# Gate and up projections by Strassen's seven products, and the out projection over two token tiles at a time

## The chip, the cores and the metric

The kernel runs on one core of one Trainium2 chip. The metric is the time of one execution on the device, in microseconds (us). The engines are TensorE (PE, with PEld for its weight loads), VectorE (DVE), ScalarE (ACT), GpSimd (POOL) and SyncE (SP), whose queue issues all DMA transfers here.

## The reference

One decoder layer for 512 tokens of width 1024, all in float32: attention and a gated recurrence are merged, then a feed-forward block. The change lies in the last three lines:

```python
merged = merge_g[:, :, 0] * (attn @ w_o_attn) + merge_g[:, :, 1] * (lru @ w_o_lru)
x = x + merged @ w_out
h2 = _rmsnorm(x, norm2_g)
return x + (jax.nn.silu(h2 @ w_gate) * (h2 @ w_up)) @ w_down
```

`w_out` is 1024 x 1024, `w_gate` and `w_up` are 1024 x 2816, `w_down` is 2816 x 1024.

## The kernel before

A float32 product is made of three matmuls of a narrower type. Each operand is split into a high part, which is the operand rounded by an ACT cast, and a low part, which is a subtraction of operand and high part; `mm3` (L193) issues high x high, high x low, low x high into one PSUM bank.

Weights come as packed chunks of 128 x 1024 (512 KB) in the order of `weight_chunks` (L65). `W.load` (L138) issues their DMA on SP into a `raw` buffer, `W.cut` (L170, L148) makes `whi` on ACT (L164) and `wlo` on DVE (L167), and `W.get` (L174) hands one over and keeps later chunks cut and loaded ahead. Everything stands in program order on each engine; nothing reorders it at run time.

The tail has three stages. The **out projection** (L1161 to L1172) keeps eight banks, four token tiles of 128 times two halves of 512 columns, and runs over the eight chunks of `w_out`; the last three chunks go token tile by token tile, so that `norm2_sums` (L1128: x added, squares on ACT, gain on POOL), `norm2_scale` (L1140) and `norm2_t` (L1147: transposes and split into `h2q`) of one tile lie beside matmuls of the next. The **gate and up projections** (L1183 to L1210) run over 22 row tiles of 128 features; each has one chunk of `w_gate` and one of `w_up`, and each chunk is multiplied with all 512 tokens in 8 x 3 matmuls of 512 columns (`mm_cm`, L283; the first three chunks take the tokens in halves of 256). Silu on ACT, the product on DVE (L1205) and a split (L1209) make the operands of the **down projection** (L1212 to L1232). Its 22 pairs stay in SBUF, as does the sum x2.

In this stage DVE and ACT make the parts two chunks ahead of PE, and POOL has nothing to do.

Of the kernel before, what the change touches and what calls it, by code (L numbers as in the profile page):

```python
# [64 lines left out]
def weight_chunks():  # L65
# [19 lines left out]
    L += [cols("w_out", ((0, D),), k, 1) for k in range(KT)]  # L85
# [14 lines left out]
def hybrid_block_kernel(ctx: ExitStack, tc: tile.TileContext, x: bass.AP, wpk: bass.AP,  # L100
# [997 lines left out]
    def late_pool(**kw):  # L1098
        p_, es = open_pool(**kw)
        ctx.enter_context(es)  # L1100
        return p_

    stage3 = late_pool(name="stage3", bufs=3, side="right")
    x2p = late_pool(name="x2p", bufs=1)
    h2p = late_pool(name="h2p", bufs=1)
    gp = late_pool(name="gp", bufs=28)
    fp = late_pool(name="fp", bufs=2, side="right")
    ps = late_pool(name="ps_ffn", bufs=8, space=PSUM)
    PS.clear()
    PS.update(b=8)  # L1110
    W.stage((stage2, stage3, stage3, stage2, stage3), (stage2, stage3), (dve,))
    x2 = x2p.tile([P, NT, D], F32, name="x2")
    for t in range(NT):
        nc.sync.dma_start(x2[:, t, :], x[t * P:(t + 1) * P, :])

    def wkey(name, h, c):
        return cols(name, ((512 * h, 512 * h + 512),), 2 * c, 2)

    h2q = [[h2p.tile([P, 4, T], F32R, name=f"h2{m}{b}") for m in "hl"] for b in range(2)]
    h2T = [[m[:, k % 4, :] for m in h2q[k // 4]] for k in range(KT)]  # L1120
    xn2, sums = {}, {}
# [24 lines left out]

    def norm2_t(t):  # L1147
        for b in range(2):
            pt = bank("b")
            for kk in range(4):  # L1150
                pe.transpose(pt[:, kk * P:(kk + 1) * P], xn2[t][b][:, kk * P:(kk + 1) * P], ident)
            split(*[m[:, :, t * P:(t + 1) * P] for m in h2q[b]], pt.rearrange("p (k n) -> p k n", n=P))

    acc = [[bank("b") for _ in range(2)] for _ in range(NT)]
# [28 lines left out]
    gT = []  # L1183
    units = [(n, i) for i in range(FT) for n in ("w_gate", "w_up")]
    early = 3
    w, acc = [], []
    for n, i in units[:early]:
        w.append(W.get(cm(n, P * i), KT, ahead=0))
        acc.append(bank("b"))
        mm_cm(acc[-1], w[-1], h2T, lo_half, between=(lambda: norm2_t(len(w))) if len(w) > 1 else None)  # L1190
    gate_acc = None
    for n, (name, i) in enumerate(units):
        if n < early:
            a = acc[n]
            mm_cm(a, w[n], h2T, hi_half)
            W.cut(W.used)
        else:
            a = bank("b")
            mm_cm(a, W.get(cm(name, P * i), KT, ahead=2), h2T)
        if name == "w_gate":  # L1200
            gate_acc = a
            continue
        sg = fp.tile([P, T], F32, tag="sg", name="sg")
        act.activation(sg, gate_acc, AF.Silu)
        dve.tensor_tensor(out=sg, in0=sg, in1=a, op=OP.mult)  # L1205
# [89 lines left out]
```

## Time and profile before

| | |
|---|---|
| runs of the kernel | 1012.01, 1012.25, 1012.58 us; median 1012.25 |
| the profiled execution | 1012.1 us, its span 1010.0 us |
| PE busy in the span | 981.0 us (97%) |
| DVE, ACT, POOL busy | 570.5 us (56%), 458.6 us (45%), 223.1 us (22%) |
| mean granted TensorE clock | 0.998 of full speed |
| DMA | 100.65 MB, mean 100 GB/s |

The span runs from the first to the last instruction of one profiled execution; the 2.1 us around it belong to the execution's time. Busy times are shares of that span, averaged over stages that differ: what a change in one stage is worth must be read there. A matmul's duration in the rows includes the time in which it overlaps the next one, so the pace of matmuls is read from their starts.

### The profile page before, as it was taken

What the parts mean: (1) busy time and instruction counts of PE and PEld (TensorE: products, weight loads), DVE (VectorE), ACT (ScalarE), POOL (GpSimd) and SP (SyncE); (2) the same over time, 40 slices, a digit from 0 to 9 for tenths busy, and PEclk for the clock granted to TensorE, in tenths of its full rate; (3) what the DMA queues carried; (4) which work ended last, traced back from release to release, by engine and by line L of the source; (5) the groups of instructions that cost most, each with busy time, mean ns of one, the idle gap of its engine ahead of it and who ended that gap; (6) DMA issues with size and microseconds to landing.
All of it is one profiled execution on the core that took longest, in us unless ns stands there. A gap on an engine that the chain in (4) does not pass through costs nothing.

```text
span 1010.0 us, 13183 instructions
## 1 busy us (share of the span) xinstructions
PE 981.0 (97%) x4915; PEld 817.0 (81%) x4915; DVE 570.5 (56%) x1053; ACT 458.6 (45%) x867; POOL 223.1 (22%) x271
## 2 busy tenths in 40 slices
PE   6999997799999999999999999999999999999998
PEld 5878876588898888778888888988888888888887
DVE  5777679746766787887875544623322332231311
ACT  6544565336545777776773334523222322231210
POOL 1031148713201555645542002200000000000000
PEclk9999999999999999999999999999999999999999
DMA  5322324642213111322113464132332233232401
GB/s 190 105 84 83 123 84 138 196 148 92 90 56 116 63 53 43 105 84 64 33 63 99 151 254 132 45 122 84 88 119 86 83 92 117 84 125 63 167 21 42
DMA packets 32175, 100.65 MB, mean 100 GB/s; under 512 B 3696, under 2 KB 4080, under 8 KB 32112
## 3 DMA queue, kind: packets, MB, share of 16 engines
q1 hardware_dynamic: 32112, 99.82, 30.7%
q8 instruction: 38, 0.62, 0.2%
q14 instruction: 25, 0.20, 0.1%
HBM read 91.42 MB, written 8.39 MB: 99 GB/s over the span
## 4 chain that ended last, share of the span: by engine, by line
PE 86%; DVE 7%; ACT 3%; issue 2%; DMA 2%; POOL 0%; ACTq 0%; DVEq 0%
PE ps_b L197 14%; PE ps_b L198 14%; PE ps_b L196 14%; PE ps_dense L1006 9%; PE ps_dense L198 5%; PE ps_dense L197 5%; PE ps_dense L196 5%; PE ps_t L880 3%; PE ps_s L197 2%; PE ps_s L196 2%; PE ps_s L198 2%; DVE wlo L167 2%; PE ps_s L849 2%; PE ps_s L850 2%; PE ps_pv L908 2%
## 5 line engine op out<-in xcount | busy, mean ns | idle before, releaser
L167 DVE TENSOR_TENSOR wlo<-raw,whi 128x1024 fp32r<-128x1024 f32 (+2 forms) x199 | 193.6, 989 | 114.0 <-ACT whi L164 113.6
L164 ACT CAST whi<-raw 128x1024 fp32r<-128x1024 f32 (+2 forms) x207 | 166.0, 819 | 136.8 <-PE ps_b L198 69.1
L196 PE MATMUL ps_b<-h2h,whi 128*128 128x512 f32 (+1 forms) x376 | 143.4, 381 | 0.0
L198 PE MATMUL ps_b<-h2h,wlo 128*128 128x512 f32 (+1 forms) x376 | 143.2, 381 | 0.0
L197 PE MATMUL ps_b<-h2l,whi 128*128 128x512 f32 (+1 forms) x376 | 143.2, 381 | 0.0
L198 PE MATMUL ps_dense<-hth,wlo 128*128 128x512 f32 (+1 forms) x232 | 87.9, 379 | 11.2 <-DVE wlo L167 11.2
L871 POOL TENSOR_SCALAR p<-p,st,gates 128x128 f32<-128x128 f32 (+3 forms) x128 | 80.0, 638 | 84.7 <-DVE st L867 47.2
L1205 DVE TENSOR_TENSOR sg<-sg,ps_b 128x512 f32<-128x512 f32 x22 | 15.2, 689 | 138.2 <-PE ps_b L198 138.2
L196 PE MATMUL ps_dense<-hth,whi 128*128 128x512 f32 (+1 forms) x232 | 87.4, 377 | 0.0
L197 PE MATMUL ps_dense<-htl,whi 128*128 128x512 f32 (+1 forms) x232 | 87.1, 375 | 0.0
L197 PEld LDWEIGHTS ps_b<-h2l,whi 128*128 128x128 f32 x376 | 70.7, 188 | 15.0
L196 PEld LDWEIGHTS ps_b<-h2h,whi 128*128 128x128 f32 x376 | 70.7, 188 | 14.9
L198 PEld LDWEIGHTS ps_b<-h2h,wlo 128*128 128x128 f32 x376 | 70.7, 188 | 14.8
L861 ACT ACTIVATE p<-p,st 128x128 f32<-128x128 f32 (+3 forms) x128 | 72.0, 563 | 23.0 <-DVE st L856 22.3
L197 PE MATMUL ps_b<-wlo,gh 128*128 128x512 f32 (+1 forms) x198 | 73.2, 370 | 0.0
L198 PE MATMUL ps_b<-whi,gl 128*128 128x512 f32 (+1 forms) x198 | 73.1, 369 | 0.0
L196 PE MATMUL ps_b<-whi,gh 128*128 128x512 f32 (+1 forms) x198 | 73.1, 369 | 0.0
L186 ACT CAST gh<-sg 128x512 fp32r<-128x512 f32 x22 | 13.6, 620 | 123.2 <-DVE sg L1205 123.2
L892 DVE TENSOR_TENSOR ptl<-ps_t,pth 128x512 fp32r<-128x512 f32 x80 | 55.1, 689 | 21.1 <-ACT pth L886 20.4
L856 DVE CUSTOM_DVE_ANT_0 p<-ps_s,bias 128x128 f32<-128x128 f32 (+3 forms) x128 | 61.2, 482 | 9.2 <-PE ps_s L850 6.2
L198 PEld LDWEIGHTS ps_dense<-hth,wlo 128*128 128x128 f32 x232 | 44.4, 191 | 21.7 <-DVE wlo L167 13.5
L886 ACT CAST pth<-ps_t 128x512 fp32r<-128x512 f32 x80 | 46.5, 582 | 29.7 <-PE ps_t L880 29.2
(265 smaller groups left out, 2072.8 us busy)
## 6 DMA issues: line engine op xcount, KB each, us to landing
raw<-in_wpk_dram SPq DMA_DIRECT2D x150, 512.0 KB, 3.6
mg_d<-mt SPq DMA_DIRECT2D x16, 256.0 KB, 4.3
mt<-mg_d SPq DMA_DIRECT2D x16, 256.0 KB, 3.0
xt<-in_x_dram SPq DMA_DIRECT2D x4, 512.0 KB, 5.6
lru_d<-lt SPq DMA_DIRECT2D x8, 256.0 KB, 5.6
lraw<-lru_d SPq DMA_DIRECT2D x8, 256.0 KB, 2.7
x<-in_x_dram SPq DMA_DIRECT2D x4, 512.0 KB, 6.5
out_dram<-o SPq DMA_DIRECT2D x7, 256.0 KB, 2.0
```

Of the source, the lines that this page charges most:

```text
L164: (on_hi or act.copy)(hi[:, sl], raw[:, sl])
L167: eng.tensor_tensor(out=lo[:, sl], in0=raw[:, sl], in1=f(hi[:, sl]), op=OP.subtract)
L196: pe.matmul(acc, lhsT=ah, rhs=bh, start=start, stop=False)
L197: pe.matmul(acc, lhsT=ah, rhs=bl, start=False, stop=False)
L198: pe.matmul(acc, lhsT=al, rhs=bh, start=False, stop=stop)
L856: dve.tensor_tensor_reduce(out=p, in0=accs.pop((h, br, t)), in1=bias[h][:, 384 - t * P:512], scale=-1.0, scalar=3e38, op0=OP.add, op1=OP.m ...
L861: act.activation(p, p, AF.Exp, bias=stat[h][:, 0, br, t:t + 1], scale=-1.0, accum_out=stat[h][:, 1, br, t:t + 1])
L871: pool.tensor_scalar(p, p, sm[:, t:t + 1], gates[:, t, c:c + 1], op0=OP.mult, op1=OP.mult)
L880: pe.transpose(pt[:, o_:o_ + P], probs[h, br, t][:, k * P:(k + 1) * P], ident)
L886: act.copy(ph, pts[h, gi][0])
L892: dve.tensor_tensor(out=pl, in0=pt, in1=f(ph), op=OP.subtract)
L1006: pe.matmul(acc, lhsT=a[l], rhs=b[r], start=start and i == 0, stop=stop and i == 2)
```

## The change

**Out projection.** The chunks of `w_out` are listed twice (`* 2`) and stored once. The first pass makes token tiles 0 and 1, the second 2 and 3, so a chunk is loaded and cut twice and serves 12 matmuls each time instead of 24. The norm of tiles 0 and 1 lies beside the second pass. x comes in by tile, the sum x2 is written to DRAM (`x2_d`) and read back near the end of each half of the down projection.

**Gate and up.** Two row tiles of both projections form a group `o`: four chunks, and with the contraction and the tokens halved, two-by-two blocks. A11 is row tile 0 with the first half of the contraction, A12 row tile 0 with the second, A21 and A22 the same for row tile 1; each has a gate part and an up part of 512 columns. B11 is the first half of the contraction for tokens 0 to 255, B21 the second half for them, B12 and B22 the same for tokens 256 to 511. Seven products take the place of eight. Four sums of A blocks (S1 to S4) are made per group on POOL, two additions of 512 columns each; the sums of B (T1 to T4) are made once. The products come in the order p = 1, 2, 6, 5, 7, 4, 3, with operands A11 x B11, A12 x B21, S2 x T2, S1 x T1, S3 x T3, A22 x T4, S4 x B22. `product` issues 2 x 4 x 3 matmuls of 256 columns into one bank, `prep` makes the parts of the weights three products ahead, `post` adds the banks up on DVE, and `gated` multiplies Silu's result on POOL. The third and fourth chunk hold A21 and A22, so S1 needs both.

**Down projection.** Its operands are kept whole and split into parts beside its own first half (`down_parts`).

The diff, cut to its core:

```diff
-    L += [cols("w_out", ((0, D),), k, 1) for k in range(KT)]
+    L += [cols("w_out", ((0, D),), k, 1) for k in range(KT)] * 2
...
+    W.raw_bufs = {id(stage2): 2, id(stage3): 3}
...
+    def blocks_late(t, pt):
+        t1, t2, t3, t4 = [half(f"t{i}") for i in range(4)]
+        act.copy(t1, pt[0])
+        dve.tensor_tensor(out=t3, in0=pt[1], in1=t1, op=OP.subtract)
+        pool.tensor_tensor(out=t2, in0=t3, in1=b11[t - 2], op=OP.add)
+        pool.tensor_tensor(out=t1, in0=t1, in1=b11[t - 2], op=OP.subtract)
+        pool.tensor_tensor(out=t4, in0=d0[t - 2], in1=t3, op=OP.subtract)
+        block("B22", t, pt[1])
+        block("T3", t, t3)
+        return (("T2", t2), ("T1", t1), ("T4", t4))
...
+    seq = [(o, p) for o in range(NO) for p in (1, 2, 6, 5, 7, 4, 3)]
...
+    SUMS = {"S1": ("A21", OP.add, "A22"), "S2": ("S1", OP.subtract, "A11"),
+            "S3": ("A11", OP.subtract, "A21"), "S4": ("A12", OP.subtract, "S2")}
+
+    def add_up(o, name):
+        S[o, name] = sp.tile([P, 1024], F32, tag="S", name="S")
+        a, op, b = SUMS[name]
+        for n in range(2):
+            pool.tensor_tensor(out=a_of(o, name, n), in0=a_of(o, a, n), in1=a_of(o, b, n), op=op)
+
+    def adds(s):
+        if s < len(seq):
+            o, p = seq[s]
+            for name in {6: ("S1", "S2"), 7: ("S3",)}.get(p, ()):
+                add_up(o, name)
...
+        if A_OF[p][0] == "S":
+            src = S.pop((o, A_OF[p])) if p != 6 else S[o, "S2"]
+            split(hi, lo, src)
+            if p == 5:
+                add_up(o, "S4")
+                load_upto(o, 6)
+            return
+        for n in range(2):
+            sl = slice(512 * n, 512 * n + 512)
+            split(hi[:, sl], lo[:, sl], a_of(o, A_OF[p], n))
+        if p == 4:
+            load_upto(o, 8)
+
+    def product(s):
+        o, p = seq[s]
+        banks[o, p] = b = at_bank(s % 8)
+        hi, lo = parts.pop(s)
+        bh, bl = h2[B_OF[p]]
+        for n in range(2):
+            for k in range(4):
+                sl = slice(512 * n + k * P, 512 * n + k * P + P)
+                mm3(b[:, 256 * n:256 * n + 256], (hi[:, sl], lo[:, sl]), (bh[:, k, :], bl[:, k, :]), k == 0, k == 3)
...
+    def gated(i, c):
+        sg = half("sg")
+        act.activation(sg, c[:, 0, :], AF.Silu)
+        pool.tensor_tensor(out=g_tile(i), in0=sg, in1=c[:, 1, :], op=OP.mult)
...
+        elif p == 6:
+            held[2] = half("u2")
+            add(both(held[2]), 6, 1)
+        elif p == 7:
+            held[3] = half("u3")
+            held[4] = half("u4")
+            add(both(held[3]), 7, 2)
+            add(both(held[4]), 5, 2)
+            add(corner(1, 1), 5, 3)
+        elif p == 4:
+            add(corner(1, 0), 4, 3)
+            gated(2 * o + 1, c2s.pop((o, 1)))
+        elif p == 3:
+            add(corner(0, 1), 3, 4)
+            gated(2 * o, c2s.pop((o, 0)))
...
+    for _ in range(KT):
+        k, w = w_out(2)
+        for t in (0, 1):
+            out_mm(t, k, w)
...
+    product(0)
+    post(0)
+    for n, src in late2:
+        block(n, 2, src)
+    pt = norm2_t(3)
+    product(1)
+    late3 = blocks_late(3, pt)
+    for n, src in late3:
+        block(n, 3, src)
+    AHEAD = 3
...
+    for s in range(2, len(seq)):
+        product(s)
+        adds(s + AHEAD + 1)
+        prep(s + AHEAD)
+        post(s - 1)
...
+            if h == 0:
+                for i in range(2 * c + 2, min(2 * c + 4, FT)):
+                    down_parts(i)
```

How the instructions stand now. **SP at the start of the out projection** (L1114, L1134 load x, L1126, L1128 the gain, L143, L145 chunks of weights, L1142 stores x2). Before:

```order
L143 DMA raw<-in_wpk_dram 128x1024
L1114 DMA x_6112<-in_x_dram 128x1024 x4
L1126 DMA gain_6121<-in_rows_dram 128x512
L1126 DMA gain_6122<-in_rows_dram 128x512
L143 DMA raw<-in_wpk_dram 128x1024 x64
```

and now:

```order
L1128 DMA gain_6113<-in_rows_dram 128x512
L1128 DMA gain_6114<-in_rows_dram 128x512
L1134 DMA x_6139<-in_x_dram 128x512
L1134 DMA x_6140<-in_x_dram 128x512
L1134 DMA x_6143<-in_x_dram 128x512
L1134 DMA x_6144<-in_x_dram 128x512
L145 DMA raw<-in_wpk_dram 128x1024 x10
L1142 DMA x_d<-x_6139 128x512
L1142 DMA x_d<-x_6140 128x512
L145 DMA raw<-in_wpk_dram 128x1024
```

Half of x stands ahead of the chunks instead of all of it, and stores of x2 stand between chunk loads.

**DVE on the way into the products**, from the end of token tile 2's norm to the first product that needs a sum of B (L189 is the subtract of `split`, L1184 is t3, L207 to L1154 the scaling of token tile 3):

```order
L189 TENSOR_TENSOR h2lB_6122<-ps_b,h2hB_6121 128x4x128
L189 TENSOR_TENSOR h2lT_6128<-t_6597,h2hT_6127 128x4x128
...
L1154 TENSOR_SCALAR xn_6581<-xn_6581,nsy 128x512
...
L1184 TENSOR_TENSOR t_6690<-ps_b,t_6688 128x512
L189 TENSOR_TENSOR h2lB_6122<-ps_b,h2hB_6121 128x4x128
L189 TENSOR_TENSOR h2lT_6128<-t_6690,h2hT_6127 128x4x128
L189 TENSOR_TENSOR h2lT_6126<-t_6689,h2hT_6125 128x4x128
L189 TENSOR_TENSOR h2lT_6124<-t_6688,h2hT_6123 128x4x128
L189 TENSOR_TENSOR h2lT_6130<-t_6691,h2hT_6129 128x4x128
L189 TENSOR_TENSOR wlo<-S,whi 128x1024 x3
```

Before, this stretch held four subtracts per token tile pair and no t; now the scaling of tile 3 stands behind tile 2's t (just ahead of these rows), B22 and T3, and the parts of S2, S1 and S3 behind all blocks of tile 3.

**A group of the gate and up projections.** Before, DVE had this from the second norm's last splits through the first row tile (L167 the subtract of one chunk, L1205 the gating, L187 the split of its result)

```order
L187 TENSOR_TENSOR h2l_6118<-ps_b,h2h_6117 128x4x128
L187 TENSOR_TENSOR h2l_6120<-ps_b,h2h_6119 128x4x128
L167 TENSOR_TENSOR wlo<-raw,whi 128x1024
L1205 TENSOR_TENSOR sg<-sg,ps_b 128x512
L187 TENSOR_TENSOR gl<-sg,gh 128x512
L167 TENSOR_TENSOR wlo<-raw,whi 128x1024 x2
```

that is, four rows for each row tile, and now it has for a group of two (L1292 are the additions of `post`; from S1 of one group to S2 of the next):

```order
L189 TENSOR_TENSOR wlo<-S,whi 128x1024
L1292 TENSOR_TENSOR c<-ps_b,u_6867 128x2x256
L189 TENSOR_TENSOR wlo<-S,whi 128x1024
L189 TENSOR_TENSOR wlo<-raw,whi 128x512 x2
L1292 TENSOR_TENSOR c<-ps_b,u_6978 128x2x256
L189 TENSOR_TENSOR wlo<-S,whi 128x1024
L1292 TENSOR_TENSOR u_7047<-ps_b,u_6978 128x512
L189 TENSOR_TENSOR wlo<-raw,whi 128x512 x4
L1292 TENSOR_TENSOR u_7117<-ps_b,u_7047 128x512
L1292 TENSOR_TENSOR u_7118<-ps_b,u_7047 128x512
L1292 TENSOR_TENSOR c<-ps_b,u_7117 128x2x256
L189 TENSOR_TENSOR wlo<-S,whi 128x1024
```

while POOL, which had nothing there, has ten operations (L1227 the sums, in the order S3, S4, S1 and S2 of the next group; L1282 the gating after p = 4 and after p = 3):

```order
L1282 TENSOR_TENSOR g<-sg,c 128x512
L1227 TENSOR_TENSOR S<-raw 128x512 x2
L1227 TENSOR_TENSOR S<-raw,S 128x512 x2
L1282 TENSOR_TENSOR g<-sg,c 128x512
L1227 TENSOR_TENSOR S<-raw 128x512 x2
L1227 TENSOR_TENSOR S<-S,raw 128x512 x2
```

DVE's row `wlo<-S` at the end is S2 of the next group; the addition after p = 4 stands behind it.

## Rows read from the trace of the kernel before

**Rows 1.** The page: busy time by engine (us, share, count), and the chain that ended last.

```profile
PE 981.0 (97%) x4915; PEld 817.0 (81%) x4915; DVE 570.5 (56%) x1053; ACT 458.6 (45%) x867; POOL 223.1 (22%) x271
...
PE 86%; DVE 7%; ACT 3%; issue 2%; DMA 2%; POOL 0%; ACTq 0%; DVEq 0%
```

**Rows 2.** Timeline of PE (start, us, engine, line): first and 36th matmul of 256 columns.

```profile
635.11 0.28 PE L196 MATMUL ps_b<-h2h,whi 128*128 128x256 f32 x1
...
639.25 0.28 PE L198 MATMUL ps_b<-h2h,wlo 128*128 128x256 f32 x1
```

**Rows 3.** The same: the last 15 matmuls of the gate and up projections, and the next.

```profile
880.00 0.40 PE L196 MATMUL ps_b<-h2h,whi 128*128 128x512 f32 x1
...
883.27 0.40 PE L198 MATMUL ps_b<-h2h,wlo 128*128 128x512 f32 x1
883.51 0.39 PE L196 MATMUL ps_b<-whi,gh 128*128 128x512 f32 x1
```

**Rows 4.** Groups by form, 660 to 880 us (busy us, mean ns | idle before).

```profile
L167 DVE TENSOR_TENSOR wlo<-raw,whi 128x1024 fp32r<-128x1024 f32 x40 | 47.2, 1222 | 5.3 <-ACT whi L164 5.3
L164 ACT CAST whi<-raw 128x1024 fp32r<-128x1024 f32 x40 | 39.9, 1045 | 0.0
L187 DVE TENSOR_TENSOR gl<-sg,gh 128x512 fp32r<-128x512 f32 x20 | 13.8, 692 | 13.7 <-ACT gh L186 13.7
L1205 DVE TENSOR_TENSOR sg<-sg,ps_b 128x512 f32<-128x512 f32 x20 | 13.8, 689 | 127.4 <-PE ps_b L198 127.4
L186 ACT CAST gh<-sg 128x512 fp32r<-128x512 f32 x20 | 12.4, 620 | 114.4 <-DVE sg L1205 114.4
L1204 ACT ACTIVATE sg<-ps_b 128x512 f32<-128x512 f32 x20 | 11.9, 598 | 46.9 <-PE ps_b L198 46.9
```

**Rows 5.** Timelines of POOL and DVE around 630 us.

```profile
629.79 2.54 POOL L1135 TENSOR_TENSOR xn<-x,gain 128x512 f32<-128x512 f32 x2 [1.20 <-DVE x L1132]
...
631.73 1.29 DVE L187 TENSOR_TENSOR h2l<-ps_b,h2h 128x512 fp32r<-128x512 f32 x2 [0.89 <-ACT h2h L186]
```

**Rows 6.** Timelines of POOL and DVE, 157 to 163 us, in the recurrence.

```profile
157.54 2.18 POOL L379 TENSOR_TENSOR tv<-tv,mv 128x512 f32<-128x512 f32 x1
...
158.58 2.23 DVE L167 TENSOR_TENSOR wlo<-raw,whi 128x1024 fp32r<-128x1024 f32 x1
...
160.72 2.30 DVE L167 TENSOR_TENSOR wlo<-raw,whi 128x1024 fp32r<-128x1024 f32 x1
```

**Rows 7.** PE's waits (total, times, longest), its timeline, and a window (last: clock, DMA).

```profile
PE ps_dense L198 <- DVE wlo L167: 11.2, 5, 5.1
...
160.86 0.80 PE L198 MATMUL ps_dense<-hth,wlo 128*128 128x512 f32 x1 [5.07 <-DVE wlo L167]
...
161.88 0.63 PE L197 MATMUL ps_dense<-htl,whi 128*128 128x512 f32 x1
162.30 0.63 PE L198 MATMUL ps_dense<-hth,wlo 128*128 128x512 f32 x1
...
162.00:163.00 1.00, 1.00 (x4) 0.81 (x3) 1.00 (x2) 0.00 (x0) 1.00 (x1) 0.50 0.53 49
```

**Rows 8.** DMA issues, 660 to 880 us (count, KB each, median us to landing).

```profile
raw<-in_wpk_dram SPq DMA_DIRECT2D x40, 512.0 KB, 3.9
```

**Rows 9.** Start of the out projection: timelines of PE, SP, ACT, and a window (last: GB/s).

```profile
588.57 0.40 PE L196 MATMUL ps_b<-whi,mh 128*128 128x512 f32 x1
...
591.03 0.48 SPq L143 DMA_DIRECT2D raw<-in_wpk_dram  x1
...
601.25 1.05 ACT L164 CAST whi<-raw 128x1024 fp32r<-128x1024 f32 x1 [8.52 <-DMA raw<-in_wpk_dram]
...
598.00:599.00 1.00, 1.00 (x6) 0.81 (x5) 0.00 (x0) 0.00 (x0) 0.00 (x0) 1.00 1.03 410
```

**Rows 10.** Timelines of DVE and ACT: the second norm of a token tile.

```profile
625.28 1.28 DVE L1132 TENSOR_TENSOR x<-x,ps_b 128x512 f32<-128x512 f32 x2
...
628.51 0.72 ACT L1144 ACTIVATE xn<-xn,nsy 128x512 f32<-128x512 f32 x1 [0.85 <-DVE nsy L208]
```

More of the change, by code (lines that the diff above doesn't have):

```diff
@@ L1099, in late_pool @@
         p_, es = open_pool(**kw)
[L1100 to L1121, printed above, removed]
+        return p_, es
+    stage3, _ = late_pool(name="stage3", bufs=3, side="right")
+    ctx.enter_context(_)
+    ga, _ = late_pool(name="ga", bufs=6)
@@ L1145, in norm2_scale, with block @@
         dve.tensor_scalar(xn2[t][1], xn2[t][1], y, None, op0=OP.mult)
+    NB = ("B11", "B21", "B22", "T1", "T2", "T3", "T4")
+    h2 = {n: [h2p.tile([P, 4, 2 * P], F32R, name=f"h2{m}{n}") for m in "hl"] for n in NB}
+    b11, d0 = {}, {}
+    def block(n, t, src):
+        sl = slice((t % 2) * P, (t % 2) * P + P)
+        split(*[m[:, :, sl] for m in h2[n]], src.rearrange("p (k n) -> p k n", n=P))
     def norm2_t(t):
+        pt = [at_bank(2 * t + b) for b in range(2)]
         for b in range(2):
-            pt = bank("b")
@@ L1150, in norm2_t, with blocks_early @@
             for kk in range(4):
[L1151 to L1154 removed]
+                pe.transpose(pt[b][:, kk * P:(kk + 1) * P], xn2[t][b][:, kk * P:(kk + 1) * P], ident)
+        return pt
+    def blocks_early(t, pt):
+        block("B11", t, pt[0])
+        block("B21", t, pt[1])
+        b11[t] = ga.tile([P, 512], F32, tag="g", name="b11")
+        d0[t] = ga.tile([P, 512], F32, tag="g", name="d0")
+        act.copy(b11[t], pt[0])
+        dve.tensor_tensor(out=d0[t], in0=pt[1], in1=b11[t], op=OP.subtract)
@@ L1180, in hybrid_block_kernel @@
-    norm2_scale(3)
[L1183 to L1195, printed above, removed]
-            W.cut(W.used)
[L1197 to L1205, printed above, removed]
-        pool_, tag = (gp, "g") if i < 14 else (hpool, "h")
-        hi = pool_.tile([P, T], F32R, tag=tag, name="gh")
-        lo = pool_.tile([P, T], F32R, tag=tag, name="gl")
-        split(hi, lo, sg)
-        gT.append((hi, lo))
+    for t in range(NT):
+        acc[t] = [at_bank(2 * t + h) for h in range(2)]
@@ new lines, in hybrid_block_kernel @@
+    ws = [w_out(late - 1 - i) for i in range(late)]
+    W.cut_ = W.used
+    W.load(W.used + 3)
+    prep(0)
+    prep(1)
+    for k, w in ws:
+        out_mm(2, k, w)
+    adds(2)
+    norm2_sums(2)
+    for k, w in ws:
+        out_mm(3, k, w)
+    norm2_scale(2)
+    pt = norm2_t(2)
+    norm2_sums(3)
+    late2 = blocks_late(2, pt)
+    norm2_scale(3)
+    product(0)
[5 more added lines that the diff above has]
+    late3 = blocks_late(3, pt)
```

178 lines of the change are left out of this document (143 added, 35 removed).

## The prediction

> **What bounds the kernel now.** I read the page first. TensorE is busy 97% of the span and the chain that ended last is 86% PE [rows 1]: PE sets the time, and whatever takes matmuls away pays in full as long as PE stays fed. The timeline of the gate and up projections comes next: the 512-column matmuls there start 14 steps apart from 880.00 to 883.27, 0.2336 us each, without gaps, and the stage ends at 883.51, where the down projection begins [rows 3]. Then, by form, the other engines in this stage: per weight chunk one ACT cast of 1.05 and one VectorE subtract of 1.22, and POOL has no row at all [rows 4]. So VectorE and ACT idle more than half of it, and POOL is free. The changed kernel spends that spare time.
>
> **Matmuls.** Before: 44 chunks x 8 x 3 = 1056 matmuls of 512 columns, 1056 x 0.2336 = 246.7 us. After: 11 groups x 7 products x 24 = 1848 of 256 columns. A narrow one is not quite half price: from 635.11 to 639.25 lie 35 steps of 256-column matmuls, each with weights of its own, 0.1183 us [rows 2]. 1848 x 0.1183 = 218.6 us. Saved: **28.1 us**. A product is 24 x 0.1183 = 2.84 us, a group 19.9; the same two row tiles took 22.4.
>
> **What each group now asks of the others.** DVE: four subtracts of 1024 (1.22) and six of 512 (0.69), seven additions that read a bank (0.69): 13.9 us. ACT: four casts of 1.05, six of 0.62, one copy and two Silu of 0.60: 9.7. POOL: eight additions for S1 to S4 and two gating multiplies; its nearest row, two 512-wide multiplies in 2.54, gives 1.27 each [rows 4, 5]: 12.7. DMA: four chunks as before, 2 MB in 20 us, where 410 GB/s were reached [rows 9]. By shares all fit under 19.9. Two things speak against reading it by shares.
>
> First, POOL and DVE stop each other when DVE reads two SBUF operands. From 157.5 on, POOL multiplies that alone take 1.27 take 2.2, and DVE subtracts that alone take 1.22 take 2.2 to 2.3, starting about 2.14 apart [rows 4 to 6]: they alternate, some 1.1 each. A DVE subtract that reads PSUM kept 1.29 for two beside the multiplies of 629.79 [rows 5]. So only the ten weight subtracts of a group collide, not its additions.
>
> The Trainium skill (SBUF — State Buffer, Who interferes with whom) says that two SBUF inputs on VectorE and a GpSimd read block each other for the whole instruction. The trace agrees that they alternate, but its 2.14 per pair is less than 1.22 + 1.27. At the full durations of rows 4 and 5 a group's colliding work is 12.7 + 4 x 1.22 + 6 x 0.69 = 21.7 us, more than PE's 19.9; by the row of the pair it is about 10 x 1.1 + 4 x 1.1 + 6 x 0.55 = 18.7, and no bound by itself. I take the row; the other is a rival below.
>
> Second, the sums form a ring from group to group. S4's last half frees the buffer into which the next group's third chunk is loaded; S1 needs that chunk, S2 needs S1, the subtract of S2 stands on DVE ahead of the addition after p=4 of the group under way (DVE's printed order), that addition feeds Silu and POOL's gating multiply, and behind the multiply POOL has S3 and S4. One turn without collisions: gating, S3, S4 on POOL 5 x 1.27 = 6.4; load 3.9 from issue to landing [rows 8]; S1 and S2 4 x 1.27 = 5.1; cast, subtract, addition, Silu 1.05 + 1.22 + 0.69 + 0.60 = 3.6: 19.0, just under PE's 19.9. Now the collisions. The subtract of S1 falls between gating and S3 (+1.1), that of S3 between S4's halves (+1.1); the four half subtracts for the next p=1 and p=2 become due just when S1 and S2 run (4 x 0.55 = +2.2); and DVE then reaches S2 late, with its last half and three additions still in front, less the cast that runs meanwhile (0.55 + 3 x 0.62 - 1.05 = +1.4). Off go 0.2 each for eight POOL operations whose start-up hides in the wait (-1.6). Sum 19.0 + 4.2 = **23.2 us a turn**. Bounds: 19.9 (nothing collides, PE sets it) and 24.8 (nothing hides). I take 23.2, because the row of the collision has the same two engines and operand kinds. Ten turns; the first finds S1 and S2 ready some 2 us early and the last group's own waits give about as much back, so nine count: 9 x (23.2 - 19.9) = **+30 us** (0 to 44).
>
> **Out projection and the way into the products.** Chunks now serve half as many matmuls: 2.8 us per chunk instead of 5.6, with cast and subtract of 1.05 and 1.22. That fits, except at the start. Before, the first chunk behind the x loads was issued at 591.03 and its cast began at 601.25, since x, gain and chunks were in flight at 410 GB/s [rows 9]; it was needed at 588.6 + 3 x 5.6 = 605.4. Now 1 MB of x is gone from the front (SP's printed order), so it lands 2.5 to 4 us earlier, but is needed at 597.0 and wants 1.05 + 1.22 first: **+2 us** (0 to 4).
>
> The tail of the norm was hidden under matmuls. From the first addition to the scaled row takes 625.28 to 629.23, about 4 us [rows 10]. Walked in the printed order of DVE, with every subtract at its row's price: in the second pass each early token tile's transposes wait about 1.2 us (DVE also cuts chunks there): 2.5. Token tile 2 starts its sums behind p=1's and p=2's subtracts and stalls PE some 2. Token tile 3 stands behind t, B22 and T3 of tile 2 (0.60 + 3 x 0.69) and its own scaling (1.9), and one product of 2.84 covers it: 4. Then product 3 needs T2 of tile 3 and S2's parts: copy, t, POOL's addition, seven subtracts of DVE (0.60 + 0.69 + 1.27 + 6 x 0.69 + 1.22 + collisions 1.5 = 9.4), covered by one product: 6.6. Sum **+15** (7 to 18). After such a gap the clock falls: a wait of 5.07 us for a subtract was followed by stretches at 0.50, the lower level, with matmuls at 0.43 instead of 0.23 for eight of them [rows 7]: **+1.6** (0 to 3.2).
>
> **At no cost.** The down projection's operands are now split during its first half: per chunk of 5.6 us DVE has 1.22 + 2 x 0.69, ACT 1.05 + 2 x 0.62; if its first two splits were late, up to 2 us. Spilling x2 adds 4 MB of traffic, and in SP's line stores that wait for DVE's additions with chunk loads behind them: those loads run two to four chunks ahead (5.6 us and more) and the additions take 1.3, so nothing, or up to 2. The last additions and stores are as before.
>
> **Sum** against the profiled execution, 1012.1 us (span 1010.0): 1012.1 - 28.1 + 30 + 2 + 15 + 1.6 = 1032.6, and 0.15 more for the median of 1012.25: **1033 us**, slower by 2%. A difference of 0.2%, 2 us, is about what can be told from none.
>
> **Rivals.** *The sums hide* (faster). If DVE seldom meets POOL, a group takes PE's 19.9 us and only the entry costs remain: 1012.2 - 28.1 + 2 + 13 + 1.6 = 1001. For it: the uncollided turn is under PE's time, and three products are prepared ahead. Against: rows 6, and the stretch around them, where DVE and POOL work without pause and PE waits 11.2 us for subtracts in five pieces [rows 7]. The point that decides: (28.1 - 18.6) / 9 = 1.06, so below 20.9 us a group it is faster, above slower. Chance 0.26.
>
> *The port alone sets the pace.* If colliding instructions exclude each other for their full durations and S2 is never late on DVE, a group is 21.7 us: 10 x 1.8 = 18, 1012.2 - 28.1 + 18 + 18.6 = 1021. For it: POOL's tail beside DVE is seen in one kind of pair only; against: 2.14 a pair [rows 6]. Chance 0.16. This is what the rule of the Trainium skill (SBUF — State Buffer, Who interferes with whom) would make of it.
>
> *Fewer matmuls do not follow.* The order of PE shows 168 narrow ones per group, so the work is removed; no chance is set aside.
>
> **How the numbers follow.** Forecast, group of 22 to 24.8 us, 1022 to 1048: 0.55. Port 0.16, hidden 0.26 (994 to 1009), worse than 1048 0.03. With some of the cheap end on either side of 1012: faster 0.27, same 0.04, slower 0.69. The range leaves out about 0.1 at each end: 997 to 1046; the forecast's own is 1020 to 1046.
>
> **What would show it.** Right: narrow matmuls still 0.118 apart within a product; PE waiting for DVE subtracts of S2, S1 and S3 in every group, with products of one kind 23 us apart; POOL additions of 2.2 us where a weight subtract overlaps and 1.3 elsewhere; two gaps of 4 to 7 us around the first two products, and a stretch at the lower clock. Wrong: groups 19.9 to 20.5 apart with PE over 95% busy, or subtracts and POOL additions that overlap unstretched.

## The result and the profile after

The changed kernel takes **1040.8 us** (median of four runs, 1038.96 to 1041.69) beside 1012.27 for the kernel before: ratio 1.0279, 95% interval 1.0262 to 1.0297, slower by 28.5 us. The profiled execution took 1040.92 us, its span 1038.9. The page of the changed kernel, busy time by engine and the chain that ended last:

```profile
PE 973.8 (94%) x5635; PEld 843.7 (81%) x5635; DVE 720.1 (69%) x1193; ACT 513.1 (49%) x962; POOL 408.9 (39%) x386
...
PE 60%; DVE 18%; issue 7%; POOL 6%; ACT 5%; DMA 3%; DVEq 0%; POOLq 0%; ACTq 0%
```

Beside [rows 1]: PE holds 60% of the chain instead of 86%, and DVE and POOL now hold 24%. PE's busy time hides this (981.0 before, 973.8 now): a narrow matmul counts for 0.28 us, though the next one starts 0.12 later, so a part of every gap counts as busy. Where the 28.9 us of span went is read from the starts on PE's timeline, here of the changed kernel:

```profile
588.65 0.39 PE L198 MATMUL ps_b<-whi,mh 128*128 128x512 f32 x1
...
646.43 0.56 PE L198 MATMUL ps_b<-h2hB,whi 128*128 128x256 f32 x1
...
680.10 0.28 PE L198 MATMUL ps_b<-h2hB,whi 128*128 128x256 f32 x1
...
682.98 0.28 PE L198 MATMUL ps_b<-h2hB,whi 128*128 128x256 f32 x1
...
700.26 0.28 PE L198 MATMUL ps_b<-h2hB,whi 128*128 128x256 f32 x1
...
722.23 0.28 PE L198 MATMUL ps_b<-h2hB,whi 128*128 128x256 f32 x1
...
885.03 0.28 PE L198 MATMUL ps_b<-h2hB,whi 128*128 128x256 f32 x1
...
908.32 0.40 PE L198 MATMUL ps_b<-whi,gh 128*128 128x512 f32 x1
...
1035.34 0.28 PE L200 MATMUL ps_b<-whi,gl 128*128 128x256 f32 x1
```

The rows are the start of the out projection, the first product, the second group's p=1 and p=2, the p=1 of the third, the fourth and the eleventh group, the start of the down projection and the last matmul. They give this table (the times of before from [rows 2, 3, 9] and its last matmul at 1006.59):

| stretch | before | after | difference |
|---|---|---|---|
| out projection, up to the first product | 46.5 | 57.8 | +11.2 |
| gate and up projections | 248.4 | 261.9 | +13.5 |
| of these: first group | | 33.7 | |
| second group; third | | 20.16; 21.97 | |
| seven groups from 722.23 to 885.03 | | 23.26 each | |
| down projection | 123.1 | 127.0 | +3.9 |

The second group had no wait: a product takes 2.88 us (680.10 to 682.98), a group 20.16. So the removed matmuls are real: 77 x 2.88 = 221.8 us stand where 246.7 stood. But the ten groups from the second on lost 26.6 us to waits (908.32 - 680.10 = 228.2, less 10 x 20.16), and the way to the second group another 23 (11.2 + 33.7 - 20.2, less the 1.7 of transposes by which 248.4 exceeds its matmuls' 246.7).

**One turn of the groups.** Timelines of POOL, then DVE, in the changed kernel:

```profile
823.26 1.29 POOL L1282 TENSOR_TENSOR g<-sg,c 128x512 f32<-128x512 f32 x1 [4.82 <-ACT sg L1281]
824.51 3.51 POOL L1227 TENSOR_TENSOR S<-raw 128x512 f32<-128x512 f32 x2
827.98 3.52 POOL L1227 TENSOR_TENSOR S<-raw,S 128x512 f32<-128x512 f32 x2
831.47 1.75 POOL L1282 TENSOR_TENSOR g<-sg,c 128x512 f32<-128x512 f32 x1
834.87 3.48 POOL L1227 TENSOR_TENSOR S<-raw 128x512 f32<-128x512 f32 x2 [1.66 <-DMA raw<-in_wpk_dram]
838.31 3.43 POOL L1227 TENSOR_TENSOR S<-S,raw 128x512 f32<-128x512 f32 x2
846.55 1.29 POOL L1282 TENSOR_TENSOR g<-sg,c 128x512 f32<-128x512 f32 x1 [4.82 <-ACT sg L1281]
```

```profile
829.13 1.22 DVE L189 TENSOR_TENSOR wlo<-S,whi 128x1024 fp32r<-128x1024 f32 x1 [2.90 <-ACT whi L188]
830.28 3.49 DVE L189 TENSOR_TENSOR wlo<-raw,whi 128x512 fp32r<-128x512 f32 x2
833.69 0.68 DVE L1292 TENSOR_TENSOR c<-ps_b,u 128x512 f32<-128x512 f32 x1
834.29 1.21 DVE L189 TENSOR_TENSOR wlo<-S,whi 128x1024 fp32r<-128x1024 f32 x1
835.42 0.68 DVE L1292 TENSOR_TENSOR u<-ps_b,u 128x512 f32<-128x512 f32 x1
836.03 6.26 DVE L189 TENSOR_TENSOR wlo<-raw,whi 128x512 fp32r<-128x512 f32 x4
842.21 1.27 DVE L1292 TENSOR_TENSOR u<-ps_b,u 128x512 f32<-128x512 f32 x2
843.41 0.67 DVE L1292 TENSOR_TENSOR c<-ps_b,u 128x512 f32<-128x512 f32 x1
844.00 1.21 DVE L189 TENSOR_TENSOR wlo<-S,whi 128x1024 fp32r<-128x1024 f32 x1
845.14 0.68 DVE L1292 TENSOR_TENSOR c<-ps_b,u 128x512 f32<-128x512 f32 x1
```

The third row of POOL is S4, the row of 834.87 is S1 of the next group and that of 838.31 its S2. POOL's gating at 823.26 waits for Silu, S3 stands behind it, the subtract of S3 is DVE's at 829.13, and from there DVE works without a pause to the subtract of the next S2 (844.00) and the addition after p=4 (845.14); Silu is at 845.85, the next gating at 846.55: 23.29 us later. The lengths 3.5 on POOL and 6.26 on DVE are collisions. Elsewhere in the same trace, DVE has the four half subtracts while POOL waits for a load for most of their time (its next sum starts at 673.83), and POOL has one half of a sum while DVE has no operand pair in SBUF (timelines of DVE and POOL):

```profile
672.05 2.49 DVE L189 TENSOR_TENSOR wlo<-raw,whi 128x512 fp32r<-128x512 f32 x4
...
827.98 1.28 POOL L1227 TENSOR_TENSOR S<-raw,S 128x512 f32<-128x512 f32 x1
```

2.49 us became 6.26; 1.28 became 1.75.

What the collisions add to this row goes into the turn one for one, as long as DVE has no pause. Two more rows of the four half subtracts, a group apart:

```profile
719.32 6.58 DVE L189 TENSOR_TENSOR wlo<-raw,whi 128x512 fp32r<-128x512 f32 x4
...
742.94 5.17 DVE L189 TENSOR_TENSOR wlo<-raw,whi 128x512 fp32r<-128x512 f32 x4
```

From the end of the first to the start of the second lie 17.04 us (742.94 - 719.32 - 6.58). Of the eight turns between 695 and 883 us six have 17.03 to 17.05 behind rows of 6.26 to 6.68 us. Behind the two short rows (5.17 and 5.19) it is 17.6: there the subtract of S2 waits some 0.5 us for its cast, and so for POOL's sum.

### The profile page after: what moved, and what is told of

Same layout as the page of the kernel before. It is cut to its first block, busy times and chain, and to the rows that moved or that the text cites. A ratio compares the mean times of both kernels' runs of the same rounds, so it can differ in the third digit from the quotient of the medians.

```text
span 1038.9 us, 15149 instructions
## 1 busy us (share of the span) xinstructions
PE 973.8 (94%) x5635; PEld 843.7 (81%) x5635; DVE 720.1 (69%) x1193; ACT 513.1 (49%) x962; POOL 408.9 (39%) x386
## 4 chain that ended last, share of the span: by engine, by line
PE 60%; DVE 18%; issue 7%; POOL 6%; ACT 5%; DMA 3%; DVEq 0%; POOLq 0%; ACTq 0%
PE ps_dense L1008 9%; DVE wlo L189 7%; PE ps_b L200 5%; PE ps_dense L200 5%; PE ps_b L199 5%; PE ps_b L198 5%; PE ps_dense L199 5%; PE ps_dense L198 5%; POOL S L1227 4%; PE ps_t L882 3%; PE ps_s L199 3%; PE ps_s L198 2%; PE ps_s L200 2%; DVE wlo L169 2%; PE ps_s L851 2%
## 5 line engine op out<-in xcount | busy, mean ns | idle before, releaser
L200 PE MATMUL ps_b<-h2hT,wlo 128*128 128x256 f32 x352 | 102.4, 291 | 15.3 <-DVE wlo L189 15.3
L198 PE MATMUL ps_b<-h2hT,whi 128*128 128x256 f32 x352 | 101.4, 288 | 11.0 <-ACT whi L188 11.0
L189 DVE TENSOR_TENSOR wlo<-raw,whi 128x512 fp32r<-128x512 f32 x66 | 100.2, 1570 | 3.6 <-ACT whi L188 3.6
L199 PE MATMUL ps_b<-h2lT,whi 128*128 128x256 f32 x352 | 99.9, 284 | 0.0
L200 PE MATMUL ps_dense<-hth,wlo 128*128 128x512 f32 (+1 forms) x232 | 89.1, 384 | 11.2 <-DVE wlo L169 11.2
L189 DVE TENSOR_TENSOR wlo<-S,whi 128x1024 fp32r<-128x1024 f32 x44 | 57.1, 1300 | 50.5 <-ACT whi L188 50.5
L1227 POOL TENSOR_TENSOR S<-raw 128x512 f32<-128x512 f32 x44 | 73.1, 1679 | 36.7 <-DMA raw<-in_wpk_dram 36.7
L200 PEld LDWEIGHTS ps_b<-h2hT,wlo 128*128 128x128 f32 x352 | 67.1, 191 | 20.3 <-DVE wlo L189 20.3
L863 ACT ACTIVATE p<-p,st 128x128 f32<-128x128 f32 (+3 forms) x128 | 72.0, 562 | 23.1 <-DVE st L858 22.4
L198 PEld LDWEIGHTS ps_b<-h2hT,whi 128*128 128x128 f32 x352 | 67.1, 191 | 13.1 <-ACT whi L188 13.1
L198 PE MATMUL ps_b<-h2hB,whi 128*128 128x256 f32 x264 | 75.1, 285 | 0.0
L200 PE MATMUL ps_b<-h2hB,wlo 128*128 128x256 f32 x264 | 74.5, 282 | 0.0
L199 PE MATMUL ps_b<-h2lB,whi 128*128 128x256 f32 x264 | 74.4, 282 | 0.0
```

Source lines behind the costliest of these rows:

```text
L189: dve.tensor_tensor(out=lo, in0=src, in1=f(hi), op=OP.subtract)
L198: pe.matmul(acc, lhsT=ah, rhs=bh, start=start, stop=False)
L199: pe.matmul(acc, lhsT=ah, rhs=bl, start=False, stop=False)
L200: pe.matmul(acc, lhsT=al, rhs=bh, start=False, stop=stop)
L863: act.activation(p, p, AF.Exp, bias=stat[h][:, 0, br, t:t + 1], scale=-1.0, accum_out=stat[h][:, 1, br, t:t + 1])
L1227: pool.tensor_tensor(out=a_of(o, name, n), in0=a_of(o, a, n), in1=a_of(o, b, n), op=op)
```

## Experiments

Each of these runs was compared with the kernel before on the same chip; medians of that were 1012.1 to 1012.6. "us a group" is the distance of two products p=1 on PE's timeline, in groups far from both ends.

**1. The gating behind S3 and S4.**

```diff
-        pool.tensor_tensor(out=g_tile(i), in0=sg, in1=c[:, 1, :], op=OP.mult)
+        pending.append((g_tile(i), sg, c[:, 1, :]))
...
         prep(s + AHEAD)
+        if s % 7 != 6:
+            gate_now()
         post(s - 1)
```

(`gate_now` issues the multiplies that are pending.)

> The changed kernel with one thing moved: the two gating multiplies stand on POOL behind S3 and S4 instead of ahead of S3 and between S4 and the next S1. The same instructions, the same work on POOL and VectorE. Ring theory (the turn from S4 over the load, S1, S2, the subtract of S2, the addition after p=4, Silu and the gating to the next S3 and S4 sets 23.3 us a group): the ring is cut, POOL has some 16.5 us of work in a group and never stands behind Silu, so PE sets the pace again, 20.2 to 21 us a group; 9 groups save 20 to 28 us, 1013 to 1021 us. Port theory (POOL and VectorE together have more colliding work than PE's time, whatever the order): the group stays at 22 to 23.3, 1029 to 1041 us.

Measured: 1036.12 us, ratio 1.0232 (1.0215 to 1.0249); 23.1 us a group. The ring theory's time did not come: the wait did not go, it moved. Waits of 730 to 900 us:

```profile
POOL S L1227 <- DVE wlo L189: 42.4, 8, 5.4
```

There are three buffers for sums, and S4 takes that of S1, whose subtract stands on DVE behind the same queue. By itself this run speaks for the port theory as well.

**2. The gating on VectorE.**

```diff
-        pool.tensor_tensor(out=g_tile(i), in0=sg, in1=c[:, 1, :], op=OP.mult)
+        dve.tensor_tensor(out=g_tile(i), in0=sg, in1=c[:, 1, :], op=OP.mult)
```

> The changed kernel with the two gating multiplies of a group on VectorE, at the same places of the program. Ring theory: POOL no longer stands behind Silu, so that edge of the ring is gone; but VectorE, busy 18.8 us of a group, takes 2 x 0.69 more and stands behind Silu itself (some 1 us each): 20.5 to 22.5 us a group, 1014 to 1034 us. Port theory: POOL's colliding work falls by 2 x 1.3 and VectorE's two-SBUF work grows by 2 x 0.69, so 1.2 us a group less: about 1030 us.

Measured: **1011.37 us**, ratio 0.9989 (0.9979 to 0.9998). One word takes the loss back, and more than was expected. PE's timeline in this kernel, p=1 of the fourth and the eleventh group, and groups by form between them:

```profile
722.23 0.28 PE L198 MATMUL ps_b<-h2hB,whi 128*128 128x256 f32 x1
...
863.35 0.28 PE L198 MATMUL ps_b<-h2hB,whi 128*128 128x256 f32 x1
```

```profile
L189 DVE TENSOR_TENSOR wlo<-raw,whi 128x512 fp32r<-128x512 f32 x42 | 46.3, 1155 | 0.0
```

141.12 / 7 = 20.16: PE sets the pace. S3 no longer stands behind Silu, so POOL does its sums earlier, and a half subtract takes 1.16 us on the mean instead of 1.66 in the changed kernel. DVE had two more operations a group and the kernel became faster: it was not DVE's amount of work that held the groups. (Its busy time fell from 18.6 to 17.3 us a group, as it collided less.)

PE keeps this pace out of a stock, though. The four half subtracts ahead of these two products p=1, on DVE's timeline:

```profile
714.31 4.59 DVE L189 TENSOR_TENSOR wlo<-raw,whi 128x512 fp32r<-128x512 f32 x4
...
857.11 6.78 DVE L189 TENSOR_TENSOR wlo<-raw,whi 128x512 fp32r<-128x512 f32 x4
```

They start 7.92 us ahead of their product in the fourth group and 6.24 in the eleventh. Between the two rows DVE takes 20.40 us a group, more than PE's 20.16: with many more groups PE would wait again.

**3. A sixth raw buffer.**

```diff
-    W.raw_bufs = {id(stage2): 2, id(stage3): 3}
+    W.raw_bufs = {id(stage2): 2, id(stage3): 4}
...
-    fp, _ = late_pool(name="fp", bufs=10)
+    fp, _ = late_pool(name="fp", bufs=9)
```

> The changed kernel with six raw buffers instead of five (and nine buffers of 512 columns instead of ten, to make room), so that the load of the third chunk need not wait for the last half of S4. If the turn runs as the prediction had it, from S4 over that load to S1 and S2, POOL's wait of 1.66 us for the load goes from every turn: 21.6 us a group, 1026 us. If it runs over VectorE's own queue instead (gating, S3, the subtract of S3 and then everything up to the subtract of the next S2 without a pause), the load is beside the path: 23.3 us, 1040 us.

Measured: 1040.34 us, ratio 1.0267 (1.0245 to 1.0289); 23.3 us a group. The edit took POOL's wait for the load away only in part. S1 in two turns, on POOL's timeline:

```profile
810.87 4.08 POOL L1227 TENSOR_TENSOR S<-raw 128x512 f32<-128x512 f32 x2 [1.05 <-DMA raw<-in_wpk_dram]
...
834.90 3.41 POOL L1227 TENSOR_TENSOR S<-raw 128x512 f32<-128x512 f32 x2 [1.72 <-DMA raw<-in_wpk_dram]
```

From gating to gating the first turn took 23.33 us (799.85 to 823.18) and the second 23.36 (823.18 to 846.54): the wait for the load differs by 0.67 us and the turn does not follow it. In both, the subtract of S2 waits for nothing but DVE's own queue. So the prediction's path over S4, the load, S1 and S2 is not the one that ends last in this kernel; the one over DVE's queue is. A run in which the load comes early in every turn was not made on this kernel.

**4. Gating later and four buffers for sums.**

```diff
-    sp, sp_es = late_pool(name="sums", bufs=3)
+    sp, sp_es = late_pool(name="sums", bufs=4)
```

on top of experiment 1, with nine buffers in `fp`.

> The kernel of the gating moved behind S3 and S4, with four buffers for sums instead of three (and nine buffers of 512 columns instead of ten). There S4 waited 5.4 us in every group, for the buffer of S1, whose subtract was late on VectorE. If the turn ran over that buffer, S4 now follows S3 at once and the group falls from 23.1 to 20.2 us: 1011 to 1015 us. If VectorE with its collisions is too slow in itself, whatever POOL waits for, the group stays at 22.5 to 23.3: 1033 to 1038 us.

Measured: 1018.29 us, ratio 1.0053 (1.0036 to 1.0071); from 719.91 to 866.47, seven groups, 20.9 us each. So the wait that experiment 1 had made was for S1's buffer, and most of it goes with a fourth; the forecast of 20.2 was too good, and the single groups take 19.8 to 22.9. POOL and VectorE have exactly the changed kernel's work here. Its colliding work at full durations is the 21.7 us of the port rival, and a group takes less: as a floor that rival falls.

**5. The out projection alone**, in the kernel before (chunks listed twice, two token tiles a pass, the second half of x loaded in the second pass):

```diff
+    for k in range(KT):
+        w = W.get(cols("w_out", ((0, D),), k, 1), 1, ahead=2)
+        for t in (0, 1):
+            out_mm(t, k, w)
```

> The kernel before with the out projection alone changed, two token tiles at a time (chunks loaded and cut twice, half of x ahead of them; the gate and up projections and the down projection as before). In the changed kernel PE waited 0.5, 1.1, 0.9 and 0.6 us for chunks in this stage, against none before. If these waits are what this half of the change costs, 1015 us. If the price is also in the norm's tail (the gap of 6.3 us before the transposes of tile 2 comes from the two passes), 1021 us; if the product parts in front of it on VectorE make that gap, none of it shows here.

Measured: 1014.45 us, ratio 1.0013 (1.0003 to 1.0023). PE's waits in this stage:

```profile
592.46 0.51 PE L196 MATMUL ps_b<-whi,mh 128*128 128x512 f32 x1 [0.30 <-ACT whi L164]
593.72 0.50 PE L197 MATMUL ps_b<-wlo,mh 128*128 128x512 f32 x1 [0.75 <-DVE wlo L167]
600.46 0.50 PE L197 MATMUL ps_b<-wlo,mh 128*128 128x512 f32 x1 [0.76 <-DVE wlo L167]
```

The last row is the fourth chunk, the one that the prediction had in mind (+2): its cast waits for the load, and PE loses 1.0 us. The first two rows are the second chunk, 1.5 us. Its load is not late; its cast (591.38 on ACT) stands behind the split of the last operand of `mT` (590.84). No gap appears ahead of tile 2's transposes. By the ratio this half of the change costs some 1.3 us, by the medians 1.9.

**6. The way into the products in another order.** The changed kernel had these gaps on PE:

```profile
644.81 1.97 PE L1170 MATMUL ps_b<-ident,xn 128*128 128x128 f32 x8 [6.19 <-ACT xn L1153]
651.43 1.10 PE L1170 MATMUL ps_b<-ident,xn 128*128 128x128 f32 x8 [1.38 <-ACT xn L1153]
661.29 0.58 PE L198 MATMUL ps_b<-h2hT,whi 128*128 128x256 f32 x1 [5.90 <-ACT whi L188]
...
664.13 0.58 PE L200 MATMUL ps_b<-h2hT,wlo 128*128 128x256 f32 x1 [2.04 <-DVE wlo L189]
```

```diff
     prep(0)
-    prep(1)
     for k, w in ws:
         out_mm(2, k, w)
-    adds(2)
     norm2_sums(2)
+    prep(1)
+    add_up(0, "S1")
...
+    diff(3)
+    prep(2)
+    block("T2", 3, tt[3][1])
```

(the other blocks of tiles 2 and 3 come behind, in the order of the products).

> The changed kernel with the way into the products written in another order: the norm of token tile 2 ahead of the weight parts of p=2, S1 and S2 on POOL behind the gain multiplies of tiles 2 and 3, T2 of both tiles and the parts of S2 ahead of the other blocks, and the weight buffers taken oldest first. The same work. If the gaps there (6.3, 2.4, 6.1 and 2.3 us, and the lower clock behind them) come from what stands ahead in the order of VectorE, POOL and ACT, the product p=6 of the first group starts at 648 to 651 us instead of 661.3, and the whole takes 1027 to 1032 us. If the chain of tile 3's norm itself is the price (4 us of norm and 4 to 5 of blocks), only the first gap goes: 1034 us or more.

Measured: 1042.76 us, ratio 1.0302 (1.0287 to 1.0318): no gain, although p=6 came 5.5 us earlier. PE's timeline in this kernel, that p=6, and p=1 of the second and the eleventh group:

```profile
655.84 0.28 PE L198 MATMUL ps_b<-h2hT,whi 128*128 128x256 f32 x1
...
677.50 0.28 PE L198 MATMUL ps_b<-h2hB,whi 128*128 128x256 f32 x1
...
887.42 0.28 PE L198 MATMUL ps_b<-h2hB,whi 128*128 128x256 f32 x1
```

Nine groups in 209.92 us: all at 23.3, from the second on. In the changed kernel POOL and DVE had used PE's long gaps to get ahead, which gave one group of 20.16 and one of 21.97. With p=6 earlier this stock is missing, and the ring sets the pace from the start. The entry's loss and the ring's are not simply added.

**7. Both together**, the entry once more reordered (`norm2_scale(2)` ahead of `prep(1)`, t2 on VectorE), and the last group's Silu behind the first operands of the down projection:

```diff
+        dve.tensor_tensor(out=tt[t][1], in0=tt[t][2], in1=b11[t - 2], op=OP.add)
...
         elif left == 1:
+            W.cut(W.used + 1)
             down_parts(0)
-        elif left == 0:
-            W.cut(W.used + 1)
             down_parts(1)
-    post(len(seq) - 1)
+    post(len(seq) - 2)
...
             wh, wl = W.get(wkey("w_down", h, c), 2, ahead=2)
+            if h == 0 and c == 1:
+                post(len(seq) - 1)
```

> The gating on VectorE (20.2 us a group), and the way into the products in another order: norm of tile 2 ahead of the parts of p=2, S1 between the gain multiplies of tiles 2 and 3, t2 on VectorE, T2 and the parts of S2 ahead of the other blocks; and the last group's Silu and gating behind the first operands of the down projection. Now the pace of the groups is PE's own, so a head start at the entry is kept: p=6 of the first group at 648 to 652 us instead of 662.6, 10 to 18 us in all with the products behind it, 1.5 us at the start of the down projection: 992 to 1000 us. If the ring comes back once the stock of sums from the long entry is missing (groups of 22 us and more), 1005 to 1015 us.

Measured: **1009.42 us, ratio 0.9968 (0.9956 to 0.9981)**, the fastest kernel here, by 0.3% below the kernel before. From the first matmul of the out projection to the second group's p=1 it takes 85.1 us, 8.0 less than in experiment 2, but the ring came back in the second group (23.3), and the later ones take 20.4, as much as DVE takes in experiment 2: the stock that had hidden it there is gone. This is the case at the other end of the forecast. Of the 8.0 us some 2 are left against experiment 2, and the two intervals still touch. Ahead of tile 3's transposes PE waits 4.21 us here, where it was 1.38 in the changed kernel.

**8. Nine buffers of 512 columns, and then six raw buffers**, each on experiment 2. The edits are those of experiment 3, one after the other.

> The kernel with the gating on VectorE, with nine buffers of 512 columns instead of ten, and nothing else: what lies behind them in SBUF, the parts of h2 and the sums among it, moves by 2 KB a partition. Where nothing waits, a product took 2.88 us with ten buffers and 2.80 in the two kernels with nine. If the place of the operands in SBUF is the reason, the groups take 19.6 us instead of 20.16 and 11 groups save 6 us: 1005 us. If the reason is something else in those kernels (the sixth raw buffer, the fourth sum), 1011 us.

> The kernel with the gating on VectorE and nine buffers of 512 columns, with six raw buffers instead of five. There a product without waits takes 2.80 us, but the groups went from 19.6 back to 20.5, with POOL waiting 4.3 us behind S4 for the load of S1 and VectorE 3.0 for S2. If that turn (S4, load, S1, S2, the subtracts of S2 and S1, S4) holds the groups, six buffers take the load out of it and the groups stay at 19.6 to 19.9: 1003 to 1006 us. If VectorE's own queue holds them, as it did in the changed kernel where the sixth buffer changed nothing, 20.4 and 1011 us.

Measured: 1011.07 us, ratio 0.9982 (0.9972 to 0.9992), and 1015.16, ratio 1.0028 (1.0017 to 1.0039). In the first, PE's narrow matmuls are faster:

```profile
680.08 0.28 PE L198 MATMUL ps_b<-h2hB,whi 128*128 128x256 f32 x1
...
682.88 0.28 PE L198 MATMUL ps_b<-h2hB,whi 128*128 128x256 f32 x1
```

2.80 us a product and 19.6 a group at first; then the groups fall back to 20.5, so the turn without the gating is some 20.5 us, above PE's new pace. Here the path over the load does end last: in eight of nine groups the subtract of S2 waits for its cast (0.47 to 2.99 us). The second run was to take the load out of that turn, and made it worse, 20.0 to 21.0 us. The four half subtracts on DVE and the sums on POOL beside them, with five raw buffers:

```profile
816.84 3.42 DVE L189 TENSOR_TENSOR wlo<-raw,whi 128x512 fp32r<-128x512 f32 x4
...
816.62 1.29 POOL L1227 TENSOR_TENSOR S<-raw 128x512 f32<-128x512 f32 x1 [4.32 <-DMA raw<-in_wpk_dram]
819.56 1.86 POOL L1227 TENSOR_TENSOR S<-raw 128x512 f32<-128x512 f32 x1 [1.65 <-DMA raw<-in_wpk_dram]
```

and with six:

```profile
838.02 6.29 DVE L189 TENSOR_TENSOR wlo<-raw,whi 128x512 fp32r<-128x512 f32 x4
...
836.68 3.67 POOL L1227 TENSOR_TENSOR S<-raw 128x512 f32<-128x512 f32 x2 [3.21 <-DMA raw<-in_wpk_dram]
840.32 3.45 POOL L1227 TENSOR_TENSOR S<-S,raw 128x512 f32<-128x512 f32 x2
```

The wait for the second chunk had kept POOL out of DVE's way. With both chunks there, POOL adds without pause beside the subtracts, and they take 6.29 us instead of 3.42. With five buffers this holds in the last four of nine turns (3.34 to 3.58 us; 5.55 to 6.74 in the others), with six the row takes 6.27 to 6.30 in seven of nine. In these seven the subtract of S2 no longer waits for its cast, and the turn is 14.66 us and the length of the row (838.02 to 858.97: 20.95). So the load went out of the path, and DVE's queue, lengthened by the collisions, took its place.

**9. More room on the kernel of experiment 7**: a fourth buffer for sums (the edit of experiment 4); the same with DVE's gating one product later (that of experiment 1, on DVE); and, instead of these, a sixth raw buffer (that of experiment 3). All have nine buffers in `fp`.

> The kernel with all reorderings, with four buffers for sums and nine of 512 columns. S4 waited 2.5 us in a group there for the buffer of S1, and the group took 20.4 us instead of 20.16. With the buffer free, POOL's turn (8 sums of 1.3 to 1.8 and the load) is under 18 us, and PE sets 19.6 to 20.2 us a group: 1000 to 1006 us. If the waits of VectorE for Silu (0.7 twice a group) set the rest, 20.2 to 20.4 us and 1006 to 1009.

> The same with the gating multiplies of VectorE one product later, so that VectorE does not stand behind Silu: 1.4 us less of waits on VectorE in a group. If VectorE's queue is what is left above PE's pace, 19.6 to 19.8 us a group, 999 to 1003 us; if not, as the kernel without this.

> The same with the other way into the products and the later last Silu. The second group took 23.3 us in the kernel with these and five raw buffers, with POOL waiting for loads, and the later ones 20.4. If the load is what holds them, 19.6 to 20 us a group from the second on, and the 6 us won at the entry are kept: 996 to 1001 us. If not, 1007 to 1010 us.

Measured: 1016.84 us, ratio 1.0036 (1.0024 to 1.0048); 1023.79, ratio 1.0106 (1.0091 to 1.0121); 1010.18, ratio 0.9982 (0.9973 to 0.9991). The first two missed both of their ranges; the third came out 0.2 us above its second one. With the sixth raw buffer the groups take 20.4 to 21.0 from the third on, as in experiment 8. With four sums most take 20.3 to 22.2, with the later gating 20.4 to 23.6 in turn. In these two POOL waits 67 us for loads between 690 and 870 us (47 in experiment 7, between 690 and 860), and the subtract of S2 waits for its cast, up to 2.98 us in most groups with four sums, and 0.47 to 2.99 in every group with the later gating: there the path over the load ends last. A sixth raw buffer was not tried with them, so this stays a reading of the traces.

## Why the prediction was right or wrong

The time fell inside the range and on the forecast's side, 8 us above the forecast. Term by term, against the profiled execution:

- **Matmuls**, -28.1: measured 246.7 - 221.8 = **-24.9**. The count was right, the pace was taken from other narrow matmuls (0.1183, [rows 2]); here a step is 2.88 / 24 = 0.1200. Experiment 8 shows that this pace changes when buffers move.
- **The ring**, +30 at 23.2 us a turn: measured **23.26 a turn, +26.6** over all groups (PE's own pace is 20.16 and not 19.9, and the second group was clean). That it is a ring and not an amount of work is shown by experiments 2 and 4. But its path was wrong in one half. "S4's last half frees the buffer into which the next group's third chunk is loaded" is true (S4 ends at 831.50, the load is issued at 831.53) and mostly beside the path (experiment 3). The path that ends last in six of eight turns goes from the gating over S3 and its subtract into DVE's own queue. Summed from the rows above: gating 1.25, S3 3.5, cast 1.05, DVE from 829.13 to 845.82, Silu and the steps between 0.8, together 23.3. The two paths share the gating, the addition after p=4 and Silu, and are nearly equally long (in the other two turns S2's cast ends last, by some 0.5 us); that the sum agrees to 0.1 us is luck, that it lies between 22 and 24.8 is not.
- **The collisions** were there, and in part as priced: S3 and S4 take 3.5 us each instead of 2.5 (1.1 more was taken for each), but the four half subtracts cost 3.8 more (6.26 - 2.49) where 2.2 was taken. DVE's subtracts and POOL's additions start 1.70 us apart (837.12, 838.82 and 840.51 within the 6.26 us row) where 0.69 and 1.27 would be 1.96 one behind the other. The Trainium skill (SBUF — State Buffer, Who interferes with whom) has the two as excluding each other; the trace agrees but for about 0.25 us of each pair. Six half subtracts a turn take 9.7 us on DVE instead of about 3.7 (2.49 for four).
- **The chunk wait**, +2: PE's steps at 591.92, 593.23, 599.81 and 633.00 came 0.5, 1.1, 0.9 and 0.6 us late, **+3.0**. The third is the chunk that was meant, and cost 0.9. The first two are the second chunk, whose cast stands on ACT (590.83) behind the split of an operand (590.29), and the last lies in the second pass; neither was in the sum.
- **Norm and blocks with the clock**, +16.6: measured about **+20**: 6.4 before tile 2's transposes, where 2 were taken; 1.5 before tile 3's instead of 4; 6.1 + 2.3 before and within p=6 instead of 6.6; none of the 2.5 for the early tiles; and some 3.3 for the lower clock instead of 1.6. The granted clock was 0.82 on the mean from 645 to 680 us, with steps of 0.21 instead of 0.12. The term that failed is tile 2's: its sums did stand behind the subtracts of p=1 and p=2, but their casts in turn waited 4.2 us for weight buffers that PE was still reading, which was not in the sum (ACT's timeline):

```profile
635.91 2.18 ACT L188 CAST whi<-raw 128x512 fp32r<-128x512 f32 x4 [4.22 <-PE ps_b L200]
```

- **Down projection**, "at no cost ... up to 2 us": **+3.9**. The Silu of the last group stands on ACT ahead of the casts of the second chunk of `w_down` and of its operands, and waits for DVE's additions behind p=4 and p=3:

```profile
913.41 0.50 PE L200 MATMUL ps_b<-whi,gl 128*128 128x512 f32 x1 [0.87 <-DVE gl L189]
```

The same wait comes once more at 917.80.

1012.1 - 24.9 + 26.6 + 3.0 + 20 + 3.9 = 1040.7. The miss of 8 us is thus matmuls 3.2, waits at the entry 4.4, the down projection 3.9, less 3.4 of the ring. The rival in which the sums hide did not come; what it needs is small, though: experiment 2 is that case for these eleven groups, by one operation on another engine and with the stock that the long entry left.

## What to carry to other kernels

Where an idle engine takes over work, follow its queue as a ring before counting its load: POOL was busy 17 of 23.3 us, and the loss came from one multiply that waited for Silu with the next sums behind it. Two engines that collide should not be fed at the same moment: more buffers made the loads early and the turn longer. A head start at the entry is worth nothing as long as a ring sets the pace behind it, and a late entry can hide a ring: in experiment 2 the engines that had got ahead of PE lost 0.24 us of their lead in each group.

## What the runs showed of the hardware

Moving what lies behind a pool by 2 KB a partition changed an unhindered product of 24 matmuls of 256 columns from 2.88 to 2.80 us, at the full granted clock and with the same instructions (experiments 2 and 8). Why was not tried. An engine that waits can be what keeps another at speed: with a load that came earlier, four half subtracts of DVE went from 3.42 to 6.29 us in the turns shown.
